# Remainders of the weights and the scale and shift of the input rows on VectorE alone

## The chip, the cores and the metric

The kernel runs on one core of a Trainium2 chip. The metric is the device time of one execution in microseconds (us); the kernel before takes 1100.27 us, the median of three runs (1099.83 to 1100.51). TensorE (PE) multiplies matrices and puts the products into PSUM; VectorE (DVE), ScalarE (ACT) and GpSimd (POOL) work on tiles elementwise; SyncE (SP) issues most DMAs, GpSimd the others.

## The reference

One step of an encoder layer, for 512 prompt tokens and 8 x 16 sample tokens (640 rows of 1024 numbers, all float32):

```
xp = layer_norm(x_prompt, ln_in_g, ln_in_b);  xs = layer_norm(x_sample, ln_in_g, ln_in_b)
mem_k = mem_prompt @ w_mem_k;  mem_v = mem_prompt @ w_mem_v
z = x @ w_in;  xa, ya, glu, q, gates = split(z)
A: h = rg_lru(conv4(xa));                     out_a = (h * gelu(ya)) @ proj_a
B: v = conv31(glu[:512] * sigmoid(glu[512:])); out_b = silu(layer_norm(v)) @ proj_b
C: attention of q over mem_k, mem_v;          out_c = ... @ proj_c
x = layer_norm(alpha * x + (sum_k sigmoid(gate_k) * out_k) @ w_out)
x = layer_norm(alpha * x + (silu(x @ w_gate) * (x @ w_up)) @ w_down)
```

The change touches the first line (the input rows' LayerNorm) and the way in which weights of the second and third lines are prepared.

## The kernel before

A product of two float32 matrices is made of three passes in a faster format. Each operand is split into a high part (a rounded copy, made by ScalarE: `copy`) and a remainder (operand minus high part, made by one `tensor_tensor` with subtract), and TensorE adds high x high, high x remainder and remainder x high. Activations are kept transposed, in `xh` and `xl` (features on partitions, 640 tokens along the row); weights come by DMA into `wr` (two buffers of 1 MB), and each step takes 128 output columns of them, high part in `wh`, remainder in `wl`, 128 x 1024 numbers each.

The program is a list of such steps (`Step`). The loop at the end of `trunk` (L1904 on) goes through them: it prepares the high parts of the two to four steps ahead, then the remainders (`prep_lo`, L301), and emits the matmuls of the step. `prep_lo` uses the engine that the step was given, `self.eng`: VectorE (`V`) as a rule, GpSimd (`G`) for some.

In order, the steps are: eight for the keys and values of the memory (`mem_steps`, L603; 128 x 512 blocks, two to a step), with the LayerNorm and the transposes of the input rows 0 to 639 (five tiles of 128 rows, `xt[0]` to `xt[4]`) put between them by a table `jobs` (L598); then from step 8 on the columns of `w_in`: four steps of GLU, four of queries, four of GLU, eight of `xa`, eight of the third gate; then `proj_c`, and so on. The first three steps of the GLU form a group: their first halves (tokens 0 to 319) run first, then the rest of the input rows is finished (`start_stream`, L557), then their second halves.

An input tile goes through `x_stats` (mean and variance on VectorE, the root on GpSimd), `x_norm` (L533: scale and shift in place; two halves y[0], y[1] of 512 columns), `x_turn` (transposes by TensorE into `pv`) and `x_split` (high part by ScalarE into `xh`, remainder by VectorE into `xl`).

What isn't in the list of steps runs in streams beside it: the convolution of branch B (`conv_b_taps`, 240 instructions of VectorE that read `pb`), its LayerNorm (`ln_b_stream`: GpSimd adds four tiles, `total`, and TensorE sums over the channels with a matrix `ones`), the attention, the recurrence. `advance` decides how much of the streams is emitted between two pieces of matmuls: it lets a stream go on while the planned time of VectorE and ScalarE is behind that of TensorE. The planned times come from prices (`price_vector`, `price_scalar`, `price_tensor`) added up by the wrapper `Engine`. Only VectorE, ScalarE and TensorE have such a wrapper; what GpSimd is given costs nothing in the plan. Each engine then runs its own queue in the order of emission and waits where an operand isn't there.

All instructions that go through the wrapper have line 64 in the profile, so they are told apart by their tiles: `s` is a general slot, `pu` and `pv` are PSUM tiles, `mv`, `rs` and `shift` are numbers of a LayerNorm for each row.

Of the kernel before, what the change touches and what calls it, by code (L numbers as in the profile page):

```python
# [11 lines left out]
OP = mybir.AluOpType  # L12
# [8 lines left out]
HT = T // 2  # L21
KD = D // 128
# [87 lines left out]
class Slots:  # L110
# [7 lines left out]
    def get(self, shape, dtype=F32):  # L118
        if not self.free_list:
            raise RuntimeError("no slot is free")  # L120
        i = self.free_list.pop(0)
        self.low = min(self.low, len(self.free_list))
        self.count += 1
        x = self.pool.tile([128, T], dtype, name=f"s{i}_{self.count}", tag=f"s{i}", bufs=1)
        x = view(x, shape)
        self.at[id(x)] = (i, x)
        return x
# [16 lines left out]
def trunk(ctx, tc, x_prompt, x_sample, mem_prompt, state_conv_a, state_lru, state_conv_b, cache_mem_k, cache_mem_v,  # L144
# [6 lines left out]
    V, A, P = Engine(nc.vector, price_vector), Engine(nc.scalar, price_scalar), Engine(nc.tensor, price_tensor)  # L151
    G, S = nc.gpsimd, nc.sync
# [20 lines left out]
    def pu(n=2):  # L173

        return [ps.tile([128, 512], F32, name="pu", tag="u", bufs=4) for _ in range(n)]
# [3 lines left out]
    def pv():  # L179
        assert side[0] < 2  # L180
        side[0] += 1
        return ps.tile([128, 2, 512], F32, name="pv", tag="v", bufs=2)
# [5 lines left out]
    def over(n=1):  # L188
        side[0] -= n


    def halves_of(p):
        return [p[:, c] for c in range(2)]

    def each(f, out, *a, **k):

        for c in range(2):
            f(c2(out)[:, c], *(x[c] if isinstance(x, list) else x for x in a), **k)

    def two(x):  # L200
        return [c2(x)[:, c] for c in range(2)]
# [16 lines left out]
    loads = []  # L218
# [44 lines left out]
    steps = []  # L263
# [83 lines left out]
    def until(cond):  # L347

        flush()
        for item in list(streams):  # L350
            while not cond():
                try:
                    next(item[1])
                except StopIteration:
                    streams.remove(item)
                    done.add(item[0])
                    break
        assert cond()
# [75 lines left out]
    mem_w = [Blocks(w_mem_k, 0)]  # L434
# [31 lines left out]
    def ln_scale(y, mv, rs):  # L466

        shift = small.tile([128, 1], F32, name="shift")
        V.scalar_tensor_tensor(shift, mv[:, 0:1], -1.0, rs, op0=OP.mult, op1=OP.mult)
        for x in y:  # L470
            A.activation(x, x, AF.Identity, bias=shift, scale=rs)
# [61 lines left out]
    def x_norm(t):  # L533
        g, b = gb_in
        mv, ve, rs = norm.pop(t)
        y = xt[t]
        ln_scale(y[1:], mv, rs)
        V.scalar_tensor_tensor(y[0], y[0], mv[:, 0:1], g[0], op0=OP.subtract, op1=OP.mult)
        V.scalar_tensor_tensor(y[0], y[0], rs, b[0], op0=OP.mult, op1=OP.add)
        G.tensor_tensor(y[1], y[1], g[1], op=OP.mult)  # L540
        G.tensor_tensor(y[1], y[1], b[1], op=OP.add)

    def x_turn(t):
        turning[t] = to_xt(t, xt[t])
# [12 lines left out]
    def start_stream():  # L557
        x_stats(4)
        yield None
        x_norm(4)  # L560
        for t in (3, 4):
            yield None
            yield from room()
            x_turn(t)
            yield None
            x_split(t)
        for r in gb_in:
            free(*r)
# [11 lines left out]
    def mem_evac(which):  # L580
# [8 lines left out]
        else:  # L589
# [5 lines left out]
            for x in memT.values():  # L595
                free(*x)

    jobs = {0: [(mem_turn, 1)], 1: [], 2: [(x_norm, 0)], 3: [(x_turn, 0), (x_stats, 1)],  # L598
            4: [(x_norm, 1), (x_split, 0), (mem_evac, "k"), (x_stats, 2)], 5: [(x_turn, 1), (x_norm, 2)],
            6: [(x_split, 1), (x_turn, 2), (x_stats, 3, False)],  # L600
            7: [(x_root, 3), (x_split, 2), (mem_evac, "v"), (x_norm, 3), (mem_end,)]}

    def mem_steps(which, li):  # L603
        for s in range(4):
            def mm(w, s=s):
                if s == 0:
                    mem_acc[which] = pu()
                p = mem_acc[which]
                for a, b in ((0, 0), (0, 1), (1, 0)):
                    for k in (2 * s, 2 * s + 1):  # L610
                        for m in range(2):
                            P.matmul(p[m], memT[m, k // 4][a][:, k % 4], w[b][:, k % 2], start=(k == 0 and a == b),
                                     stop=(k == KD - 1 and a == 1))
                yield
                for f, *a in jobs[li + s]:
                    f(*a)

            Step(mem_w[li + s], lambda r: r, [128, 2, 512], mm, eng=G if li + s in (3, 5) else V)

    mem_steps("k", 0)  # L620
    mem_steps("v", 4)

    us = {}
# [70 lines left out]
    def fm(p, w, rh, rl, K, cs=(0, 1)):  # L694
        hi, lo = w
        for k in range(K):
            for c in cs:
                P.matmul(p[c][:, :HT], hi[:, k], rh(k, c), start=(k == 0), stop=False)
            for c in cs:
                P.matmul(p[c][:, :HT], hi[:, k], rl(k, c), start=False, stop=False)  # L700
            for c in cs:
                P.matmul(p[c][:, :HT], lo[:, k], rh(k, c), start=False, stop=(k == K - 1))
            if k % 2 == 1:
                yield k % 4 == 1
# [15 lines left out]
    def x_step(ld, o, evac, group=None):  # L720

        def mm(w):
            if group is None:
                s.p = pu()
                yield from fm(s.p, w, xrh, xrl, KD)
                return
            if group[1][0] is s:
                until(lambda: {0, 1, 2} <= turned)
                for z, q in enumerate(group[1]):
                    if z == 2:  # L730
                        until(lambda: side[0] < 2)
                    q.p = pu() if z < 2 else halves_of(pv())
                    yield from fm(q.p, q.w, xrh, xrl, KD, (0,))
                group[0]()
            if s is group[1][-1]:
                over()
            yield from fm(s.p, w, xrh, xrl, KD, (1,))

        s = Step(ld, lambda r: r[:, :, o:o + 128], [128, KD, 128], mm, lambda: evac([x[:, :HT] for x in s.p]),
                 eng=G if ld is loads[0] and o == 0 or 12 <= len(steps) < 36 and len(steps) % 2 else V)  # L740
        if group is not None:
            group[1].append(s)

    def z_step(col, evac, group=None):
        o = col % 256
        x_step(zload[col - o], o, evac, group)
# [984 lines left out]
    for which in ("g", "u"):  # L1731
        for m in range(2):
            def evac(p, m=m, which=which):
                if which == "g":
                    hT[m] = get([128, T])
                    each(A.activation, hT[m], p, AF.Silu)
                else:
                    each(V.tensor_mul, hT[m], two(hT[m]), p)

            x_step(zload[which], m * 128, evac, group=group if len(group[1]) < 3 else None)  # L1740
# [218 lines left out]
```

## Time and profile before

| | |
|---|---|
| median of three runs | 1100.27 us |
| the profiled execution | 1099.67 us |
| its span, first to last instruction | 1097.9 us |
| TensorE busy | 1061.7 us, 97% |
| VectorE busy | 802.9 us, 73% |
| ScalarE busy | 490.1 us, 45% |
| GpSimd busy | 165.3 us, 15% |
| mean granted TensorE clock | 0.99 |

The profile is of one execution. A row of the timeline reads: start in us from the span's start, duration in us, engine, line, operation, output<-inputs, shape, number of instructions merged into the row, and in brackets how long the engine had idled before and what ended that. TensorE's durations overlap (a matmul of 320 columns lasts 0.31 us and the next one starts 0.147 us after it), so its busy time says little; its waits and the granted clock tell where it loses time.

### The profile page before, as it was taken

To read this page: it belongs to the slowest core of one execution; us is meant where nothing else is said; L and a number is where in the kernel's file an instruction comes from. 1 tells how busy PE (TensorE), PEld (TensorE's weight loads), DVE (VectorE), ACT (ScalarE), POOL (GpSimd) and SP (SyncE) were. 2 spreads that over 40 slices of the span, in tenths; PEclk is the share of its full clock that TensorE was granted. 3 is DMA by queue.
4 is the path that set the end of the run, shared out by engine and by line. 5 is a ranking of instruction groups with operands and counts; after the bars stand their busy time and mean duration, and the time that the engine had idled before them with its cause. 6 is when DMAs were issued, how large, how long until landed. Compare 5 with 4: busy or idle time off the path is not lost.

```text
span 1097.9 us, 17000 instructions
## 1 busy us (share of the span) xinstructions
PE 1061.7 (97%) x6827; PEld 1005.9 (92%) x6827; DVE 802.9 (73%) x1335; ACT 490.1 (45%) x863; POOL 165.3 (15%) x185
## 2 busy tenths in 40 slices
PE   8799898998999999999999999899999999999997
PEld 6699898997999999999999889899999999888886
DVE  6929898996364873779855678888887887544775
ACT  4532645446648445846523124433444444334341
POOL 3623323556200000010001120000000000100111
PEclk9999999998999999999999999999999999999999
DMA  9732123352412121212325331132222322734481
GB/s 340 253 95 78 39 67 97 118 154 65 147 52 83 59 96 59 95 45 78 115 78 172 135 134 59 39 101 92 77 78 85 108 77 78 287 115 137 162 289 45
DMA packets 80334, 123.11 MB, mean 112 GB/s; under 512 B 4075, under 2 KB 59371, under 8 KB 80256
## 3 DMA queue, kind: packets, MB, share of 16 engines
q1 hardware_dynamic: 73168, 100.36, 27.6%
q0 software_dynamic: 7088, 21.68, 6.2%
q8 instruction: 53, 0.87, 0.3%
q14 instruction: 25, 0.20, 0.1%
HBM read 112.41 MB, written 9.61 MB: 111 GB/s over the span
## 4 chain that ended last, share of the span: by engine, by line
PE 70%; DVE 11%; ACT 4%; issue 1%; DVEq 0%; ACTq 0%
PE pu L64 62%; DVE s L64 10%; PE pv L64 8%; ACT s L64 3%; ACT L64 1%; DVE wl L64 1%; ACT wh L64 0%; DVE xres L64 0%; DVE mx L64 0%; DVE wh L64 0%; DVE xl L64 0%; DVE nm L64 0%; DVEq L1955 0%; ACT wl L64 0%; DVE st L64 0%
## 5 line engine op out<-in xcount | busy, mean ns | idle before, releaser
L64 PE MATMUL pu<-xh,wh 128*128 128x320 f32 x1040 | 252.6, 315 | 8.3 <-ACT s L64 7.1
L64 PE MATMUL pu<-xh,wl 128*128 128x320 f32 x1040 | 246.9, 310 | 0.0
L64 ACT ACTIVATE wh<-wr 128x1024 fp32r<-128x1024 f32 (+1 forms) x149 | 134.9, 908 | 229.1 <-PE pu L64 123.2
L64 PE MATMUL pu<-xl,wh 128*128 128x320 f32 x888 | 219.7, 311 | 0.0
L64 PEld LDWEIGHTS pu<-xh,wh 128*128 128x128 f32 x1040 | 178.1, 190 | 13.2 <-ACT s L64 9.1
L64 PE MATMUL pu<-s,wh 128*128 128x320 f32 x1064 | 185.5, 310 | 1.9 <-DVE s L64 1.3
L64 PEld LDWEIGHTS pu<-xh,wl 128*128 128x128 f32 x1040 | 177.4, 189 | 0.1
L64 DVE TENSOR_TENSOR s<-s,s 128x640 fp32r<-128x640 f32 (+4 forms) x176 | 124.5, 723 | 65.5 <-ACT s L64 63.3
L64 PEld LDWEIGHTS pu<-s,wh 128*128 128x128 f32 x1064 | 163.4, 188 | 3.4 <-DVE s L64 2.4
L64 DVE TENSOR_TENSOR wl<-wr,wh 128x1024 fp32r<-128x1024 f32 (+1 forms) x100 | 114.1, 1141 | 66.7 <-ACT wh L64 66.7
L64 PEld LDWEIGHTS pu<-xl,wh 128*128 128x128 f32 x888 | 154.2, 189 | 0.6 <-DVE xl L64 0.6
L64 DVE TENSOR_TENSOR s<-s,pu 128x320 f32<-128x320 f32 x188 | 88.4, 484 | 85.8 <-PE pu L64 83.3
L64 PE MATMUL pu<-s,wl 128*128 128x320 f32 x808 | 147.3, 310 | 0.9 <-DVE s L64 0.9
L64 DVE SCALAR_TENSOR_TENSOR s<-s,pb,s 128x511 f32<-128x511 f32 (+14 forms) x240 | 130.1, 613 | 7.8 <-ACT s L64 7.8
L64 ACT ACTIVATE s<-s 128x640 fp32r<-128x640 f32 (+4 forms) x144 | 87.9, 629 | 101.9 <-DVE s L64 101.8
L64 PEld LDWEIGHTS pu<-s,wl 128*128 128x128 f32 x808 | 126.1, 188 | 1.1 <-issue 1.1
L64 PE MATMUL pu<-wh,s 128*128 128x512 f32 (+1 forms) x396 | 116.2, 386 | 0.3 <-ACT wh L64 0.3
L64 PEld LDWEIGHTS pu<-wh,s 128*128 128x128 f32 x396 | 73.1, 189 | 15.1 <-ACT wh L64 1.2
L64 ACT ACTIVATE s<-pu 128x320 f32<-128x320 f32 (+2 forms) x90 | 36.7, 442 | 68.1 <-PE pu L64 68.0
L64 PE MATMUL pu<-wl,s 128*128 128x512 f32 (+1 forms) x198 | 62.9, 389 | 1.6 <-POOL wl L305 0.8
L305 POOL TENSOR_TENSOR wl<-wr,wh 128x1024 fp32r<-128x1024 f32 x13 | 44.4, 3418 | 81.2 <-ACT wh L64 68.4
L64 PE MATMUL pv<-wh,s 128*128 128x512 f32 (+1 forms) x152 | 48.7, 367 | 0.4 <-DVE xres L64 0.4
(139 smaller groups left out, 1249.0 us busy)
## 6 DMA issues: line engine op xcount, KB each, us to landing
wr<-in_w_in SPq DMA_DIRECT2D x26, 1024.0 KB, 5.1
wr<-in_w_ffn_down SPq DMA_DIRECT2D x19, 1024.0 KB, 5.1
wr<-in_w_ffn_gate SPq DMA_DIRECT2D x11, 1024.0 KB, 5.3
wr<-in_w_ffn_up SPq DMA_DIRECT2D x11, 1024.0 KB, 5.3
s<-in_cache_mem_k POOLq DMA_DIRECT2D x16, 256.0 KB, 7.0
s<-in_cache_mem_v POOLq DMA_DIRECT2D x16, 256.0 KB, 7.2
wr<-in_proj_a SPq DMA_DIRECT2D x4, 1024.0 KB
wr<-in_w_out SPq DMA_DIRECT2D x4, 1024.0 KB, 5.7
```

The lines of the kernel that those rows point to most:

```text
L64: return f(*a, **k)
L305: self.eng.tensor_tensor(l, x, f32(h), op=OP.subtract)
```

## The change

Three edits. In `x_norm`, both halves of an input tile are now scaled and shifted by two VectorE instructions each; before, y[1] was scaled by one ScalarE instruction (with a number `shift` that VectorE computes first) and then multiplied by g and added to b by GpSimd. In `mem_steps`, steps 3 and 5 no longer give their remainders to GpSimd. In `x_step`, the first step of `w_in` and the twelve odd steps from 13 to 35 no longer do so either.

```
@@ -534,11 +534,9 @@  x_norm
-        ln_scale(y[1:], mv, rs)
-        V.scalar_tensor_tensor(y[0], y[0], mv[:, 0:1], g[0], op0=OP.subtract, op1=OP.mult)
-        V.scalar_tensor_tensor(y[0], y[0], rs, b[0], op0=OP.mult, op1=OP.add)
-        G.tensor_tensor(y[1], y[1], g[1], op=OP.mult)
-        G.tensor_tensor(y[1], y[1], b[1], op=OP.add)
+        for c in range(2):
+            V.scalar_tensor_tensor(y[c], y[c], mv[:, 0:1], g[c], op0=OP.subtract, op1=OP.mult)
+            V.scalar_tensor_tensor(y[c], y[c], rs, b[c], op0=OP.mult, op1=OP.add)
@@ -615,7 +613,7 @@  mem_steps
-            Step(mem_w[li + s], lambda r: r, [128, 2, 512], mm, eng=G if li + s in (3, 5) else V)
+            Step(mem_w[li + s], lambda r: r, [128, 2, 512], mm)
@@ -736,8 +734,7 @@  x_step
-        s = Step(ld, lambda r: r[:, :, o:o + 128], [128, KD, 128], mm, lambda: evac([x[:, :HT] for x in s.p]),
-                 eng=G if ld is loads[0] and o == 0 or 12 <= len(steps) < 36 and len(steps) % 2 else V)
+        s = Step(ld, lambda r: r[:, :, o:o + 128], [128, KD, 128], mm, lambda: evac([x[:, :HT] for x in s.p]))
```

Since the plan counts VectorE's instructions and not GpSimd's, the streams are also laid out anew between the steps. Three places matter for what follows.

VectorE's queue at memory step 3, before (`s_13_117` and `s_14_118` are the two blocks of that step, done by GpSimd and so not in these rows; `s_7_103` and `s_8_104` are the halves of input tile 0, `s_19_129` is a block of step 4):

```order
L64 TENSOR_TENSOR wl<-s_12_114,wh 128x512
L64 SCALAR_TENSOR_TENSOR shift<-mv,rs 128x1
L64 SCALAR_TENSOR_TENSOR s_7_103<-s_7_103,mv,s_15_121 128x512
L64 SCALAR_TENSOR_TENSOR s_7_103<-s_7_103,rs,s_17_125 128x512
L64 TENSOR_TENSOR wl<-s_19_129,wh 128x512
```

and with the change:

```order
L64 TENSOR_TENSOR wl<-s_12_114,wh 128x512
L64 TENSOR_TENSOR wl<-s_13_117,wh 128x512
L64 TENSOR_TENSOR wl<-s_14_118,wh 128x512
L64 SCALAR_TENSOR_TENSOR s_7_103<-s_7_103,mv,s_15_121 128x512
L64 SCALAR_TENSOR_TENSOR s_7_103<-s_7_103,rs,s_17_125 128x512
L64 SCALAR_TENSOR_TENSOR s_8_104<-s_8_104,mv,s_16_122 128x512
L64 SCALAR_TENSOR_TENSOR s_8_104<-s_8_104,rs,s_18_126 128x512
L64 TENSOR_TENSOR wl<-s_19_129,wh 128x512
```

Both halves of the tile and both blocks of the step now stand in one queue, ahead of the next step's remainders.

ScalarE's queue at the first two softmaxes of the attention, before (rows with `nm` are the exponentials of a row tile, rows with `rc` their scaling, a row into `s` from `pu` empties a step's PSUM tiles, ACT_TABLE_LOAD changes the function table, the row with `pb` starts a convolution):

```order
L64 ACT_TABLE_LOAD
L64 ACTIVATE lam_1261<-lam_1260 128x8
L64 ACTIVATE s_74_1297,sm<-pv,nm 128x256 x2
L64 ACTIVATE s_75_1298,sm<-pv,nm 128x256 x2
L64 ACTIVATE s_76_1316<-s_60_763,pb 128x640
L64 ACT_TABLE_LOAD
L64 ACTIVATE s_77_1326<-pu 128x320 x2
L64 ACTIVATE s_74_1297<-s_74_1297,rc 128x256 x2
L64 ACTIVATE s_75_1298<-s_75_1298,rc 128x256 x2
L64 ACT_TABLE_LOAD
L64 ACTIVATE s_78_1367,sm<-pv,nm 128x256 x2
L64 ACTIVATE s_79_1368,sm<-pv,nm 128x256 x2
```

and with the change, to the row that empties the next step:

```order
L64 ACT_TABLE_LOAD
L64 ACTIVATE lam_1280<-lam_1279 128x8
L64 ACTIVATE s_76_1316,sm<-pv,nm 128x256 x2
L64 ACTIVATE s_77_1317,sm<-pv,nm 128x256 x2
L64 ACTIVATE wh<-wr 128x1024
L64 ACTIVATE s_76_1316<-s_76_1316,rc 128x256 x2
L64 ACTIVATE s_77_1317<-s_77_1317,rc 128x256 x2
L64 ACTIVATE s_78_1379,sm<-pv,nm 128x256 x2
L64 ACTIVATE s_79_1380,sm<-pv,nm 128x256 x2
L64 ACT_TABLE_LOAD
L64 ACTIVATE s_80_1391<-pu 128x320 x2
```

The convolution's start and the emptying of one step now stand ahead of the first exponentials, and one pair of table loads is gone; the whole queue has 19 table loads, before 25.

TensorE's queue where branch B's first channel sums stand (the matmuls with `ones`; `s_162_2714` is the sum of the four convolved tiles made by GpSimd, the rows with `s_95` and `s_96` are score products of the samples), before:

```order
L64 MATMUL pv<-s_160_2700,s_96_1828 32x256
L64 MATMUL pv<-s_161_2702,s_96_1828 32x256
...
L64 MATMUL pv<-s_162_2714,ones 128x512
L64 MATMUL pv<-s_162_2714,ones 128x128
```

and with the change (`s_162_2719` and `s_163_2720` are now probabilities of the samples, `s_155_2619` to `s_158_2622` cached values, `s_181_2871` the sum of the convolved tiles):

```order
L64 MATMUL pv<-ident,s_162_2719 128x128 x4
L64 MATMUL pv<-ident,s_163_2720 128x128 x4
...
L64 MATMUL pv<-s_157_2621,s_179_2854 32x128
L64 MATMUL pv<-s_158_2622,s_179_2854 32x128
L64 MATMUL pv<-s_181_2871,ones 128x512
L64 MATMUL pv<-s_181_2871,ones 128x128
```

The sums stood right behind the score products and now stand behind the samples' softmax and their first value products. Ahead of them TensorE's queue has 1176 matmuls of 320 columns, before 1080. Behind the place where the transposes of `hout` (the end of the recurrence) stood before, TensorE's queue is the same in both programs.

## The prediction

> **What bounds the kernel now.** The page first:
>
> ```profile
> PE 1061.7 (97%) x6827; PEld 1005.9 (92%) x6827; DVE 802.9 (73%) x1335; ACT 490.1 (45%) x863; POOL 165.3 (15%) x185
> DVE  6929898996364873779855678888887887544775
> L305 POOL TENSOR_TENSOR wl<-wr,wh 128x1024 fp32r<-128x1024 f32 x13 | 44.4, 3418 | 81.2 <-ACT wh L64 68.4
> ```
>
> TensorE sets the time: no edit touches its matmuls, so only its waits and slow clock can be won or lost. VectorE's digits are 8 and 9 in slices 2 and 4 to 9 (27 to 247 us, 27.4 us each): there it is nearly full, and there the change adds work to it. The third line is what leaves GpSimd: 13 remainders at 3.42 us. Next, TensorE's waits from 60 to 260 us, and stretches of that time:
>
> ```profile
> PE pv L64 <- POOL s L855: 5.0, 1, 5.0
> PE pu L64 <- ACT s L64: 2.3, 1, 2.3
> PE pu L64 <- DVE s L64: 1.0, 1, 1.0
> ...
> 138.00:142.00 4.00, 4.00 (x19) 4.00 (x18) 4.00 (x7) 1.75 (x5) 3.34 (x1) 0.58 0.00 0
> 220.00:240.00 20.00, 20.00 (x162) 18.47 (x161) 20.00 (x39) 9.98 (x20) 10.76 (x9) 1.00 0.54 159
> 248.00:252.00 4.00, 0.17 (x2) 0.00 (x0) 4.00 (x9) 0.00 (x0) 0.42 (x1) 0.82 0.00 0
> 252.00:256.00 4.00, 2.83 (x7) 1.80 (x7) 2.23 (x3) 2.78 (x8) 4.00 (x5) 0.50 0.34 93
> 256.00:260.00 4.00, 4.00 (x24) 4.00 (x24) 1.76 (x5) 3.97 (x9) 3.46 (x7) 0.83 0.97 288
> ```
>
> (A stretch's columns: length, busy us of PE, PEld, DVE, ACT and POOL with counts, granted clock, DMA share, GB/s.) From 248 us TensorE stands still for 5.0 us: the `ones` matmul waits for GpSimd's sum of the convolved tiles, while VectorE, 20.00 of 20.00 busy before, finishes the last one. Then the clock is at half until about 257.
>
> **What GpSimd's work costs VectorE.** Rows of VectorE in the front, and the undisturbed kind at 32.50 to 34:
>
> ```profile
> 15.74 1.25 DVE L64 SCALAR_TENSOR_TENSOR shift<-mv,rs 128x1 f32<-128x1 f32 x1
> 16.91 1.86 DVE L64 SCALAR_TENSOR_TENSOR s<-s,mv,s 128x512 f32<-128x512 f32 x1
> 18.80 1.66 DVE L64 SCALAR_TENSOR_TENSOR s<-s,rs,s 128x512 f32<-128x512 f32 x1
> 20.39 2.35 DVE L64 TENSOR_TENSOR wl<-s,wh 128x512 fp32r<-128x512 f32 x2
> 25.03 1.23 DVE L64 SCALAR_TENSOR_TENSOR shift<-mv,rs 128x1 f32<-128x1 f32 x1 [0.66 <-POOL rs L463]
> 26.19 1.85 DVE L64 SCALAR_TENSOR_TENSOR s<-s,mv,s 128x512 f32<-128x512 f32 x1
> 28.08 1.67 DVE L64 SCALAR_TENSOR_TENSOR s<-s,rs,s 128x512 f32<-128x512 f32 x1
> 32.50 1.29 DVE L64 TENSOR_TENSOR wl<-s,wh 128x512 fp32r<-128x512 f32 x2
> 33.71 0.15 DVE L64 SCALAR_TENSOR_TENSOR shift<-mv,rs 128x1 f32<-128x1 f32 x1
> 33.78 0.74 DVE L64 SCALAR_TENSOR_TENSOR s<-s,mv,s 128x512 f32<-128x512 f32 x1
> 35.26 3.41 DVE L64 TENSOR_TENSOR wl<-s,wh 128x512 fp32r<-128x512 f32 x2
> 41.43 1.23 DVE L64 TENSOR_TENSOR wl<-wr,wh 128x1024 fp32r<-128x1024 f32 x1
> ```
>
> The same forms take 0.74 us in one place and 1.86 in another, a `shift` of one number a row 0.15 or 1.25. All long ones lie over GpSimd's `wl`, L540 and L541. Their excess: 1.10 + 1.12 + 0.92 + 1.06 + 1.08 + 1.11 + 0.93 + 2.12 = 9.4 us up to 39 us. In the middle (the last row counts only what reads the taps' table `pb`: busy us of DVE and of ACT):
>
> ```profile
> 198.58 3.80 POOL L305 TENSOR_TENSOR wl<-wr,wh 128x1024 fp32r<-128x1024 f32 x1 [11.04 <-ACT wh L64]
> 200.03 2.88 DVE L64 SCALAR_TENSOR_TENSOR s<-s,pb,s 128x495 f32<-128x495 f32 x1
> 204.91 0.72 DVE L64 SCALAR_TENSOR_TENSOR s<-s,pb,s 128x492 f32<-128x492 f32 x1
> 107.83 6.37 DVE L64 SCALAR_TENSOR_TENSOR s<-s,pb,s 128x490 f32<-128x490 f32 x14
> 178.00:252.00 74.00, 67.17 (x120) 1.49 (x2) 0.99 0.45 133
> ```
>
> One remainder on GpSimd holds one tap up by 2.88 - 0.72 = 2.16 us. VectorE does a remainder itself in 1.23 (row 41.43). So for each of these VectorE pays less when it does the work than when GpSimd does. The stretch agrees: 120 taps took 67.2 us; at 6.37/14 = 0.455 they would take 54.6; of the 12.6 us between, four remainders make 4 x 2.16 = 8.6, the rest falls on GpSimd's own adds, which stay.
>
> The page "Perfetto Trace Analysis" of the Trainium skill ("Optimizing Scalar/DVE Operations") says that with VectorE saturated, offloading to ScalarE or even GpSimd may make sense; the change does the reverse in a full stretch. It adds that between GpSimd and VectorE this may not help because of a shared read port; the rows above bear out the second half.
>
> **The change, part by part.** The sum is made against the profiled execution's 1099.67 us (span 1097.9 and 1.8 around it), which is 0.6 us below the runs' median.
>
> *A, the front (to 58 us).*
>
> ```profile
> 38.17 0.66 PE L64 MATMUL pv<-ident,s 128*128 128x128 f32 x4 [2.09 <-POOL s L541]
> 38.00:40.00 2.00, 1.83 (x8) 1.58 (x9) 2.00 (x4) 1.70 (x3) 2.00 (x2) 0.73 0.98 327
> 40.00:42.00 2.00, 2.00 (x6) 1.52 (x6) 1.93 (x5) 0.00 (x0) 1.35 (x2) 0.50 0.74 276
> 43.31 0.41 PE L64 MATMUL pu<-xl,wh 128*128 128x320 f32 x1
> 49.98 0.66 PE L64 MATMUL pv<-ident,s 128*128 128x128 f32 x4 [0.84 <-POOL s L541]
> 54.90 1.37 PE L64 MATMUL pv<-ident,s 128*128 128x128 f32 x8 [0.74 <-DVE xl L64]
> 57.87 0.31 PE L64 MATMUL pu<-xh,wh 128*128 128x320 f32 x1
> ```
>
> VectorE is full from 14.5 us, and the first matmul with `xl` (43.31) waits for it. Its queue up to there gains two pairs of blocks (2 x 1.29), two 0.75 instructions for each of tiles 0 to 2 (4.5) and one remainder (1.23): 8.3 us. It loses the excess, 9.4, and three `shift`s, 0.4. Net -1.5: the `xl` matmul at 41.8. ScalarE's and GpSimd's lost work there (five of each) lay beside VectorE's and gives no more. TensorE now reaches that matmul early: its memory steps no longer wait for L541, tile 2's second half is ready near 34.7 rather than at 38.1 (VectorE's queue again), and transposes and the last step take 3.9 us from there, so they end near 38.6 and TensorE idles some 3 us. A wait of 2.09 us (row 38.17) was followed by 3.4 us of half clock, 1.7 us lost; I charge 1.3 of the same here, part of it lying inside the wait. From the `xl` matmul to the second halves' start was 57.87 - 43.31 = 14.6 us, with waits of 0.84 at 49.98 and 0.74 at the next tile. The first goes: behind the `xl` pair VectorE has one more pair and tile 3's four instructions, 1.3 + 3.0 us, done by 47. The second grows: with the new order no matmuls stand between tile 4's transposes and the second halves, so ScalarE's copy and VectorE's remainder of its first half are waited for in full, about 0.6 us each (half of the pair's 1.29, and as much for the copy), 0.4 more than before. 41.8 + 1.3 + 14.6 - 0.84 + 0.4 = 57.2 against 57.87: **A = -0.7**; bounds -2.5 (no half clock, tile 4 hidden) and +1.5 (a second half-clock period at tile 4).
>
> "TensorE: Matmul & The Clock Gate" of the Trainium skill (Part 1) gives at least one idle window of about 3.4 us before the clock halves. By that rule the idle 3 us need not halve it and A would be -2.0. The row after 2.09 us of waiting speaks against counting on it, so the charge stays.
>
> *B, the stop at 248 us.* GpSimd's adds, and from the chain of work a stretch of matmuls without waits (start, us, count):
>
> ```profile
> L855 POOL TENSOR_TENSOR s<-s,s 128x640 f32<-128x640 f32 x4 | 6.7, 1674 | 11.1 <-DVE s L64 8.1 <-ACT s L64 2.9
> 293.90 12.32 PE pu L64 x84
> ```
>
> The stop is 5.0 us of wait and, from its end at 253.2 to about 257, half clock on some 3.6 us, 1.8 us. With the change the `ones` matmul stands 96 matmuls of 320 columns later in TensorE's queue, 96 x 12.32/84 = 14 us. VectorE in the same stretch has 4 x (2.16 - 1.23) = 3.7 us less to do, and 2 x 1.23 = 2.5 us more for the two steps that now fall into it. So the last tap is done before TensorE arrives. What is late next is GpSimd's three adds, 1.7 us each: before, two were done ahead of the last tap; now all stand behind it, and there are 3.5 us of matmuls plus the transposes and value products between emission and use, where 5.1 are needed. I leave 1.5 us of wait, below the 2.09 that is followed by half clock. **B = -5.0 - 1.8 + 1.5 = -5.3**; bounds -6.8 and 0.
>
> *C, 107 us.* The 1.0 us wait for a VectorE row stands behind taps lengthened by GpSimd's remainder of 100.5 us. **C = -1.0**; bounds -1.0 and 0.
>
> *D, 137 us.*
>
> ```profile
> 130.85 1.28 ACT L64 ACT_TABLE_LOAD   x1 [0.48 <-DVE nm L64]
> 133.96 1.07 ACT L64 ACTIVATE wh<-wr 128x1024 fp32r<-128x1024 f32 x1
> 136.82 0.74 PE L64 MATMUL pu<-xh,wh 128*128 128x320 f32 x2 [2.30 <-ACT s L64]
> ```
>
> TensorE waits 2.3 us until ScalarE, after two softmaxes with a table load between, empties the step's PSUM; half clock follows (0.58 from 138 to 142), 1.7 us. In the new queue the load at 130.85 (1.28) and the copy at 133.96 (1.07) no longer stand in that chain: 2.35 us, as much as the wait. **D = -4.0**; bounds -4.0 and 0, since the softmax keeps its place on ScalarE and a wait may return there.
>
> *E, VectorE's new work elsewhere.* Eleven remainders at 1.23 us join its queue from 60 to 285 us. Where it has room, they lie beside matmuls; at a softmax or the emptying of a step one may stand ahead of what TensorE waits for. I charge one, **+1.2**; bounds -2 (small waits go, as VectorE is freer) and +5 (four in the full stretch, as in the rival below). Weight buffers come free sooner, which hides nothing, since no matmul waits there for a weight's DMA.
>
> Sum: -0.7 - 5.3 - 1.0 - 4.0 + 1.2 = -9.8: **1089.9 us**; the case's own range is 1084 to 1095.
>
> **The rivals.**
> 1. *The stop moves.* The wait of B returns on GpSimd's adds (5 us behind the last tap, half clock again), or D's returns at another softmax. For it: both have a new neighbour that is nearly as late. Against: neither wait needs VectorE's backlog any more. Time: 1089.9 + 4.0 to 5.3, about 1094.5.
> 2. *Both return.* 1089.9 + 9.3 = 1099.2, no difference. That the change did nothing by itself, because GpSimd wasn't in the way, would end there too; the 0.74 against 1.86 speaks against it.
> 3. *VectorE becomes the bound.* In the full stretch 180 to 250 us four remainders at 1.23 stand ahead of taps and of the emptying of steps, with nothing given back: 4.9 us more, 1104.6, slower. It decides if a tap beside a remainder shrinks by less than 1.23 us; the 2.16 measured, and 14 us more room in TensorE's queue, speak against. The rule on a saturated VectorE in "Perfetto Trace Analysis" (the Trainium skill), cited above, would come out this way.
>
> **How the numbers follow.** Forecast 0.55, rival 1 0.20, rival 2 0.10, rival 3 0.15. A measurement of this kernel can tell about 0.2% (2.2 us) from no change: forecast and rival 1 are faster, 0.75; rival 2 same, 0.10; rival 3 slower, 0.15. The low end takes the terms' best bounds but part of E: 1099.7 - 2.5 - 6.8 - 1 - 4 - 2 = 1083.4. The high end, 1101, takes in rivals 1 and 2 and leaves out most of rival 3.
>
> **What would show it.** Right: VectorE's busy time near the old one (26 us added: 13 remainders at 1.23, 4 at 0.65, ten instructions of 0.75; gone the 9.4 and about ten times 2.16), taps of 0.72 everywhere but under GpSimd's adds; the `xl` matmul near 41.8; a wait below 2 us at `ones`; no half clock near 137 and 250; the second halves starting near 57. Wrong: forms of 0.74 us still taking 1.8 with GpSimd idle; `ones` waiting 3 us or more; new waits of TensorE for VectorE's `s` or `wl` between 60 and 260 us, or clock halved at 55.

## The result and the profile after

| | before | after |
|---|---|---|
| median, us | 1100.39 (four runs, 1099.83 to 1101.31) | 1083.04 (four runs, 1080.89 to 1084.34) |
| profiled execution, us | 1099.67 | 1080.89 |
| its span, us | 1097.9 | 1078.8 |

The ratio is 0.9841, 95% interval 0.9828 to 0.9854: 17.3 us faster. The forecast was 1089.9, with a range from 1083.4 to 1101: the gain is larger than forecast, and the time lies 0.4 us below the range. The profiled execution is the fastest of the four.

From the page of after, the busy times of the engines, VectorE's digits and the group of the convolution's taps:

```profile
PE 1052.7 (98%) x6827; PEld 1002.7 (93%) x6827; DVE 798.6 (74%) x1357; ACT 479.4 (44%) x852; POOL 107.8 (10%) x158
DVE  6939989988377747877545678888878887545775
L64 DVE SCALAR_TENSOR_TENSOR s<-s,pb,s 128x511 f32<-128x511 f32 (+14 forms) x240 | 112.6, 540 | 2.8 <-ACT s L64 2.8
```

The same group on the page of before:

```profile
L64 DVE SCALAR_TENSOR_TENSOR s<-s,pb,s 128x511 f32<-128x511 f32 (+14 forms) x240 | 130.1, 613 | 7.8 <-ACT s L64 7.8
```

VectorE has 22 instructions more, 13 of them remainders of 1.2 us, and yet is busy for 4.3 us less; the 240 taps alone took 17.5 us less. From 178 to 252 us the taps now read (busy us of VectorE second, with its count):

```profile
178.00:252.00 74.00, 52.28 (x111) 0.92 (x1) 1.00 0.51 151
```

That is 0.471 us for one, against 67.17/120 = 0.560 before. TensorE's waits between 60 and 300 us in after (total us, times, longest):

```profile
PE pv L64 <- ACT s L64: 1.4, 2, 0.9
PE pu L64 <- ACT s L64: 0.6, 1, 0.6
PE pu L64 <- DVE s L64: 0.4, 1, 0.4
```

and the stretch from 100 to 200 us in after:

```profile
100.00:200.00 100.00, 100.00 (x718) 99.90 (x717) 93.34 (x200) 52.88 (x142) 27.45 (x49) 1.00 0.36 109
```

In before the same list of waits, the lines that the prediction did not show:

```profile
PE pv L64 <- DVE s L64: 2.6, 3, 1.6
...
PE pv L64 <- ACT s L64: 1.1, 1, 1.1
```

and the same stretch in before:

```profile
100.00:200.00 100.00, 92.93 (x639) 90.81 (x638) 89.99 (x181) 51.65 (x136) 29.62 (x43) 0.98 0.22 67
```

Between 100 and 200 us TensorE no longer waits at all: 718 matmuls where there were 639, and a granted clock of 1.00 where it was 0.98. The places that the prediction named, in after's timeline:

```profile
41.66 0.42 PE L64 MATMUL pu<-xl,wh 128*128 128x320 f32 x1 [3.33 <-DVE xl L64]
...
55.25 0.41 PE L64 MATMUL pu<-xh,wh 128*128 128x320 f32 x1 [0.69 <-ACT xh L64]
56.46 0.42 PE L64 MATMUL pu<-xl,wh 128*128 128x320 f32 x1 [0.81 <-DVE xl L64]
...
234.48 2.02 POOL L852 TENSOR_TENSOR s<-s,s 128x640 f32<-128x640 f32 x1
248.35 4.04 POOL L852 TENSOR_TENSOR s<-s,s 128x640 f32<-128x640 f32 x1 [11.85 <-DVE s L64]
```

and the `ones` matmuls among after's instructions by tile (shortest, median and longest ns, first and last start us):

```profile
L64 PE MATMUL pv<-s,ones x4: 273/434/697, 253.3 to 254.3; 128*128 128x512 f32 x2, 128*128 128x128 f32 x2
```

The first matmul with `xl` waits 3.33 us; the `ones` matmuls start 0.9 us after GpSimd's last add has ended (248.35 + 4.04) and wait for nothing.

Where the time was gained is seen by pairing the k-th matmul of 320 columns into `pu` of two traces and taking the difference of their starts. Between 240 and 480 us the pairing is disturbed, since other matmuls moved across these, so columns are taken outside of it. At 119 us the kernels with the order of after (all rows but e1) have 12 matmuls of 256 columns still to come that before has behind it, about 1.5 us of what they show there; in the other columns the matmuls ahead are the same. The kernels of the experiments below are in the same table.

| us gained, at the time in before | 64 | 119 | 205 | 235 | 491 | 930 |
|---|---|---|---|---|---|---|
| after | 1.7 | 6.2 | 12.7 | 12.7 | 18.9 | 19.1 |
| e1: VectorE does the work, order of before | 1.5 | 2.8 | 5.7 | 5.8 | 9.3 | 9.7 |
| e2: GpSimd does the work, order of after | -0.3 | 4.2 | 10.6 | 3.3 | 3.7 | 4.0 |
| e10: e2 with one remainder on VectorE | 0.1 | 4.6 | 11.0 | 11.0 | 10.9 | 11.6 |
| e4: the twelve odd steps alone | -0.1 | 4.4 | 10.8 | 10.8 | 17.0 | 17.6 |
| e5: after, with idle subtractions on GpSimd | -0.9 | 3.6 | 8.2 | 8.2 | 3.0 | 2.0 |

After gains 1.7 us in the front, 11.0 from 64 to 205 us, 6.4 behind that. The middle is the surprise: its forecast was C + D + E = -3.8.

### The profile page after: what moved, and what is told of

It reads as the page before. It is cut to its first block, busy times and chain, and to the rows that moved or that the text cites. A ratio compares the mean times of both kernels' runs of the same rounds, so it can differ in the third digit from the quotient of the medians.

```text
span 1078.8 us, 16991 instructions
## 1 busy us (share of the span) xinstructions
PE 1052.7 (98%) x6827; PEld 1002.7 (93%) x6827; DVE 798.6 (74%) x1357; ACT 479.4 (44%) x852; POOL 107.8 (10%) x158
## 4 chain that ended last, share of the span: by engine, by line
PE 54%; DVE 1%; ACT 0%; issue 0%; DVEq 0%; ACTq 0%
PE pu L64 48%; PE pv L64 6%; DVE s L64 1%; DVE xres L64 0%; ACT s L64 0%; ACT wh L64 0%; DVEq L1952 0%; ACT wl L64 0%; DVE st L64 0%; DVE mv L64 0%; DVE ve L64 0%; DVE wl L64 0%; ACTq L64 0%; DVEq L64 0%
## 5 line engine op out<-in xcount | busy, mean ns | idle before, releaser
L64 DVE TENSOR_TENSOR wl<-wr,wh 128x1024 fp32r<-128x1024 f32 (+1 forms) x113 | 130.1, 1152 | 62.6 <-ACT wh L64 62.5
L64 DVE SCALAR_TENSOR_TENSOR s<-s,pb,s 128x511 f32<-128x511 f32 (+14 forms) x240 | 112.6, 540 | 2.8 <-ACT s L64 2.8
L64 PE MATMUL pv<-s,s 128*32 128x128 f32 (+4 forms) x420 | 45.8, 308 | 1.4 <-ACT s L64 1.4
```

Of the source, the lines that this page charges most:

```text
L64: return f(*a, **k)
```

## The experiments

The change does two things at once: another engine does the work, and the plan, which counts VectorE's instructions and not GpSimd's, lays out the streams anew. Theory 1: the gain comes from VectorE no longer being held up by GpSimd's subtractions. Theory 2: it comes from the new order. The first two kernels separate them. Times are medians; the ratio with its 95% interval is against runs of before on the same chip (medians 1099.9 to 1100.0).

| | us | ratio |
|---|---|---|
| e1_vector_old_layout | 1090.22 | 0.9917 (0.9902 to 0.9932) |
| e2_gpsimd_new_layout | 1095.51 | 0.9965 (0.9953 to 0.9977) |
| e3_norm_only | 1100.55 | 1.0012 (1.0003 to 1.0022) |
| e4_odd_steps_only | 1081.95 | 0.9839 (0.9823 to 0.9856) |
| e5_idle_subtractions | 1096.51 | 0.9962 (0.9948 to 0.9975) |
| e6_idle_memsets | 1083.80 | 0.9850 (0.9834 to 0.9867) |
| e7_front_order | 1081.44 | 0.9830 (0.9816 to 0.9845) |
| e9_gpsimd_keys_by_sync | 1096.72 | 0.9967 (0.9955 to 0.9978) |
| e10_one_remainder_back | 1087.73 | 0.9889 (0.9872 to 0.9905) |

**e1: the engine alone.** VectorE does all of it, but past the wrapper that counts its time, so that TensorE's queue is that of before:

```
-            Step(mem_w[li + s], lambda r: r, [128, 2, 512], mm)
+            Step(mem_w[li + s], lambda r: r, [128, 2, 512], mm, eng=nc.vector if li + s in (3, 5) else V)
...
+                 eng=nc.vector if ld is loads[0] and o == 0 or 12 <= len(steps) < 36 and len(steps) % 2 else V)
...
+        V.time += 130 + 1 / 0.96
+        A.time += 130 + 512 / 1.2 + 2 * 93
+            v = nc.vector if c else V
+            v.scalar_tensor_tensor(y[c], y[c], mv[:, 0:1], g[c], op0=OP.subtract, op1=OP.mult)
+            v.scalar_tensor_tensor(y[c], y[c], rs, b[c], op0=OP.mult, op1=OP.add)
```

> VectorE does all remainders and both halves of every input tile, but the plan is charged as before, so TensorE's and ScalarE's queues are those of the kernel before (ScalarE without its five scalings). Hold-up theory (GpSimd's instructions stretch VectorE's, and TensorE waits for the stretched ones): nearly the whole gain comes with the engine alone, 1083 to 1087 us. Layout theory (the streams placed later between the steps win the time): VectorE's rows shorten, but the waits stay where they stood; only the front's 1 to 2 us go, 1096 to 1099 us.

Measured: 1090.22 us, 9.1 of the 17.3 us by the ratio, between the two ranges expected. Two of TensorE's waits in its timeline:

```profile
134.66 0.74 PE L64 MATMUL pu<-xh,wh 128*128 128x320 f32 x2 [2.95 <-ACT s L64]
...
243.87 1.35 PE L64 MATMUL pv<-s,ones 128*128 128x512 f32 x4 [1.46 <-POOL s L856]
```

all of TensorE's waits from 100 to 200 us:

```profile
PE pu L64 <- ACT s L64: 3.0, 1, 3.0
PE pv L64 <- DVE s L64: 1.2, 2, 0.9
```

and its taps from 178 to 252 us:

```profile
178.00:252.00 74.00, 54.20 (x113) 0.92 (x1) 1.00 0.50 151
```

The taps are as short as in after. The stop at `ones` shrinks from 5.0 to 1.46 us. From 100 to 200 us TensorE waits for 4.2 us, 7.0 in before: the waits of before at 107 (0.98), 169 (1.15) and 188 us (1.62) are gone. But the wait of term D is still there, longer than the 2.30 before: taking GpSimd out of VectorE's way does not remove it.

**e2: the order alone.** GpSimd and ScalarE keep their work, and its time is added to the plan as if VectorE did it, so that TensorE's queue is that of after:

```
+    class GV:
+        @staticmethod
+        def tensor_tensor(*a, **k):
+            V.time += price_vector(V, "tensor_tensor", a, k)
+            return G.tensor_tensor(*a, **k)
...
+            Step(mem_w[li + s], lambda r: r, [128, 2, 512], mm, eng=GV if li + s in (3, 5) else V)
...
+                 eng=GV if ld is loads[0] and o == 0 or 12 <= len(steps) < 36 and len(steps) % 2 else V)
...
+        V.time += 2 * (130 + 512 / 0.96)
```

> GpSimd and ScalarE keep their work as before, but the plan is charged as in the changed kernel, so TensorE's queue is the changed kernel's. Hold-up theory: the stretched rows stay, 1095 to 1102 us. Layout theory: 1084 to 1089 us. If both shares are needed, this run and the first one add up to more or less than the 17 us together.

Measured: 1095.51 us, 3.8 us by the ratio. That lies in the range expected of theory 1. Its trace shows why the number is small, and it is not for stretched rows of VectorE alone. First the stretch from 100 to 200 us:

```profile
100.00:200.00 100.00, 100.00 (x717) 99.90 (x717) 92.13 (x194) 53.24 (x145) 45.22 (x51) 1.00 0.30 94
```

then rows of TensorE, GpSimd and VectorE in its timeline:

```profile
227.58 1.09 PE L64 MATMUL pv<-ident,s 128*128 128x128 f32 x4 [4.76 <-DMA s<-in_cache_mem_k]
...
265.14 1.94 PE L64 MATMUL pv<-s,s 128*32 128x128 f32 x32 [5.06 <-ACT s L64]
...
203.79 18.37 POOL L158 TENSOR_TENSOR wl<-wr,wh 128x1024 fp32r<-128x1024 f32 x1 [6.99 <-PE pv L64]
222.10 2.99 POOL L1078 DMA_DIRECT2D s<-in_cache_mem_k  x4
...
202.28 16.47 DVE L64 SCALAR_TENSOR_TENSOR s<-s,pb,s 128x488 f32<-128x488 f32 x36
```

Up to 205 us the order alone gains 10.6 us, nearly what after has there (12.7, of which 1.7 came in the front), although GpSimd still does its subtractions. Then two waits of about 5 us come. By the table the first takes back 7.3 us (from 10.6 to 3.3); the second stands where before has its own stop of 5.0 us, so that nothing is won there. One GpSimd remainder lasts 18.37 us; during it VectorE runs 36 taps at 16.47/36 = 0.457 us, not held up at all, and the loads of cached keys that GpSimd issues stand behind it.

**e3 and e4: which of the edits.** e3 has only the edit in `x_norm`, e4 only the one that gives the twelve odd steps from 13 to 35 to VectorE.

```
-                 eng=G if ld is loads[0] and o == 0 or 12 <= len(steps) < 36 and len(steps) % 2 else V)
+                 eng=G if ld is loads[0] and o == 0 else V)
```

> Only the scale and shift of the input rows goes to VectorE; remainders stay on GpSimd. Hold-up theory: the front loses five scalings and ten GpSimd instructions, so 1 to 2 us go before 64 us, and all later waits stay: 1097 to 1100 us. Layout theory: the plan moves little, the same time; this run tells what share the front has, not which theory holds.

> Only the twelve odd steps from 13 to 35 give their remainders to VectorE; the front is the kernel before's. Both theories: the 15 us between 64 and 300 us go, the front's 2 us stay: 1083 to 1087 us. If it is above 1092 us, the front's edits also work behind 64 us.

Measured: e3 1100.55, no gain and just above its range; e4 1081.95, the whole gain and 1 us below its range. TensorE's waits from 60 to 300 us in e4:

```profile
PE pv L64 <- ACT s L64: 1.4, 2, 0.9
PE pu L64 <- ACT s L64: 0.6, 1, 0.6
```

They are those of after but for one of 0.4 us. The front edits bring nothing measurable: up to 60 us VectorE is busy for 45.72 us in before and for 45.40 in after, so what the hold-ups cost there, its new work costs again.

**e5 and e6: the hold-up by itself.** To after are added, at each of the twelve odd steps, instructions of GpSimd whose result nobody uses: two subtractions of 128 x 512 in e5, six memsets of 128 x 512 in e6.

```
+            i = steps.index(self)
+            if 12 <= i < 36 and i % 2:
+                for k in range(2):
+                    G.tensor_tensor(scr, f32(xh[:, k, :512]), f32(xl[:, k, :512]), op=OP.subtract)
...
+    scr = one.tile([128, 512], F32, name="scr")
```

> The changed kernel, with two extra GpSimd subtractions of 128x512 at each of the twelve odd steps (operands xh and xl, result never read): GpSimd is as busy as before, nobody waits for it, queues and plan of the other engines are the changed kernel's. Hold-up theory: VectorE's rows lengthen again (24 times about 1.1 us) or GpSimd's do, and the late GpSimd DMAs and adds come later: 1086 to 1094 us. If the time lay only in waiting for GpSimd's results: 1082 to 1085 us, as the changed kernel.

> The same, with six memsets of 128x512 (0.53 us each, 3.2 us a step) in the place of the two subtractions: GpSimd is busy as long but reads nothing. If VectorE is held up by any GpSimd instruction, as in the run with subtractions. If it is held up only by those that read two tiles, VectorE's rows stay short and the time is the changed kernel's within 2 us.

Measured: e5 1096.51, 13.5 us above after and above the range expected; e6 1083.80, as after. GpSimd's group of the added instructions from 60 to 300 us (busy us, mean ns, idle time before them) in e5:

```profile
L309 POOL TENSOR_TENSOR scr<-xh,xl 128x512 f32<-128x512 f32 x21 | 33.6, 1598 | 1.2
```

e5's taps from 178 to 252 us:

```profile
178.00:252.00 74.00, 63.73 (x110) 0.92 (x1) 0.96 0.51 153
```

and in e5's timeline VectorE's row that gives the softmax of the samples its maximum, with ScalarE and TensorE behind it:

```profile
248.63 0.17 DVE L64 TENSOR_SCALAR nm<-mx 128x4 f32<-128x4 f32 x1
...
248.88 1.28 ACT L64 ACT_TABLE_LOAD   x1 [12.81 <-DVE nm L64]
...
254.00 1.05 PE L64 MATMUL pu<-xh,wh 128*128 128x320 f32 x2 [10.50 <-ACT s L64]
```

The same table load in after:

```profile
234.51 1.28 ACT L64 ACT_TABLE_LOAD   x1 [2.93 <-DVE nm L64]
```

The group of the added instructions in e6:

```profile
L309 POOL MEMSET scr<- 128x512 f32 x62 | 32.7, 528 | 3.2
```

and e6's taps:

```profile
178.00:252.00 74.00, 54.33 (x116) 0.92 (x1) 1.00 0.49 146
```

GpSimd is busy for as long in both (33.6 and 32.7 us). Beside the subtractions a tap takes 63.73/110 = 0.579 us, beside the memsets 54.33/116 = 0.468, in after 0.471. Subtractions of SBUF tiles hold VectorE up, memsets don't. In the full stretch the delay adds up until ScalarE idles 12.81 us for `nm`, where it idles 2.93 in after, and TensorE stands for 10.50 us.

The Trainium skill, page "SBUF — State Buffer", section "Who interferes with whom", says that a VectorE instruction with two inputs in SBUF contends with a GpSimd instruction that reads SBUF, not with one that only writes it. e5 and e6 agree: 0.579 and 0.468 us.

**e7: the front's wait.** After, with tile 3's statistics and the remainder of step 9 moved behind tile 2's split, so that `xl` is ready earlier.

```
-            6: [(x_split, 1), (x_turn, 2), (x_stats, 3, False)],
-            7: [(x_root, 3), (x_split, 2), (mem_evac, "v"), (x_norm, 3), (mem_end,)]}
+            6: [(x_split, 1), (x_turn, 2)],
+            7: [(x_split, 2), (lambda: steps[9].prep_lo(),), (x_stats, 3), (mem_evac, "v"), (x_norm, 3), (mem_end,)]}
...
-            while new:
+            while new and not (i == 7 and len(new) == 1):
```

> The changed kernel with tile 3's statistics and step 9's remainder put behind the xl pair of tile 2 in VectorE's queue (same work, same TensorE queue). The 3.3 us wait for xl at 41.7 us shrinks to under 1 us. If that wait is what the front loses: 1079 to 1081 us. If VectorE's sum of work up to the second halves bounds the front, the wait returns at step 10's remainder or tile 4, and the time is 1081 to 1084 us, but for the half-clock period that a 3.3 us wait brings in some executions.

Measured: 1081.44 (1080.52 to 1082.47). In its timeline:

```profile
38.93 0.41 PE L64 MATMUL pu<-xl,wh 128*128 128x320 f32 x1 [0.55 <-DVE xl L64]
49.27 0.41 PE L64 MATMUL pv<-xh,wl 128*128 128x320 f32 x1 [1.86 <-DVE wl L64]
...
55.86 0.41 PE L64 MATMUL pu<-xh,wh 128*128 128x320 f32 x1 [0.69 <-ACT xh L64]
```

and a stretch of the front (the granted clock is the third number from the end):

```profile
50.00:54.00 4.00, 4.00 (x19) 4.00 (x19) 3.34 (x5) 0.00 (x0) 3.90 (x8) 0.57 0.93 331
```

The wait of 3.33 us is gone, another of 1.86 us for VectorE comes at the next step, as in the second outcome expected, and the second halves start at 55.86, in after's profiled execution at 55.25. But half clock followed the new wait (0.57 from 50 to 54 us), so this trace doesn't show whether VectorE's sum alone bounds the front. Its median is 1.6 us below after's, 0.15%, which these runs don't tell from no change.

**e9 and e10: what takes back the gain of e2.** e9 is e2 with the loads of cached keys and values issued by SyncE, so that they don't stand behind GpSimd's remainders.

```
-                G.dma_start(to[h][i], rows[:, 4 * i:4 * i + 4, h])
+                S.dma_start(to[h][i], rows[:, 4 * i:4 * i + 4, h])
```

> GpSimd keeps the work, the plan is the changed kernel's (the second run), and the DMAs of the cached keys and values are issued by SyncE. The second run's 4.8 us wait for a cached key stood behind one GpSimd remainder of 18.4 us. If the queue behind that remainder is the cause: the wait goes, 1086 to 1091 us. If the transfer itself was late, or SyncE's queue holds it as long, 1094 to 1098 us.

Measured: 1096.72, no better than e2, and TensorE still waits for the keys: the second of the two outcomes expected. TensorE, SyncE's queue and GpSimd in its timeline:

```profile
228.18 1.94 PE L64 MATMUL pv<-ident,s 128*128 128x128 f32 x8 [5.36 <-DMA s<-in_cache_mem_k]
...
194.26 3.76 SPq L1078 DMA_DIRECT2D s<-in_cache_mem_k  x4
222.19 0.37 SPq L265 DMA_DIRECT2D wr<-in_w_in  x1
222.60 3.22 SPq L1078 DMA_DIRECT2D s<-in_cache_mem_k  x4
...
203.78 18.38 POOL L158 TENSOR_TENSOR wl<-wr,wh 128x1024 fp32r<-128x1024 f32 x1 [13.32 <-PE pv L64]
```

SyncE issues nothing from 198 to 222.19 us. The weight load at its head writes a buffer `wr`, and the long remainder reads one until 203.78 + 18.38 = 222.16, just before the load goes out. By these times the keys stand behind the same instruction on either queue. e10 tries this: e2, with only that one remainder (step 29) given to VectorE; all queues are else in the same order.

```
-                 eng=GV if ld is loads[0] and o == 0 or 12 <= len(steps) < 36 and len(steps) % 2 else V)
+                 eng=GV if ld is loads[0] and o == 0 or 12 <= len(steps) < 36 and len(steps) % 2 and len(steps) != 29 else V)
```

> As e2_gpsimd_new_layout, but the remainder of one step, the one that lasted 18.37 us on GpSimd at 203.79, is made by VectorE; the order of all queues is else the same. Theory (the stop at 227 us comes from that one long subtraction, which holds up the issue of the cached keys on GpSimd's own queue, and with the keys on SyncE's queue holds up SyncE through the weight buffer): the keys go out before 215 us, the wait of 4.76 us for in_cache_mem_k is gone, the next GpSimd remainder at 228 is ordinary, and the time is 1086 to 1090 us (1095.5 - 4.8 - 1.7 of half clock - up to 3 of what follows). Rival (the keys are late since the streams are emitted too late whatever GpSimd does, or another remainder starves in its place): a wait of over 3 us for in_cache_mem_k stays between 220 and 235, and the time is 1094 to 1097 us.

Measured: 1087.73, 7.8 us below e2, from one instruction. In its timeline:

```profile
201.38 0.75 POOL L1078 DMA_DIRECT2D s<-in_cache_mem_k  x1 [1.63 <-DMA s<-in_cache_mem_k]
204.99 2.96 POOL L1078 DMA_DIRECT2D s<-in_cache_mem_v  x4 [2.86 <-ACT s L64]
223.34 10.46 POOL L158 TENSOR_TENSOR wl<-wr,wh 128x1024 fp32r<-128x1024 f32 x1 [15.38 <-ACT wh L64]
...
257.52 1.94 PE L64 MATMUL pv<-s,s 128*32 128x128 f32 x32 [5.10 <-ACT s L64]
```

The keys go out by about 202 us and the wait for them is gone. The next remainder was expected to be an ordinary one and took 10.46 us; the second wait of e2 stays (5.10 us). That one makes up most of the 5.8 us between e10 and e4, which has the same work but no GpSimd remainder in the full stretch; the chain that leads to it through VectorE and ScalarE was not tried apart.

## Where the prediction was right, and where it failed

The direction was right, and so was the hold-up: GpSimd's subtractions cost VectorE more than the work itself does. Eight of them lie in e5's stretch from 178 to 252 us, and against e6 its taps lose about 110 x (0.579 - 0.468) = 12 us there, 1.5 us for each, where VectorE makes two such blocks in 1.29. The stop at 248 us hung on VectorE's backlog (5.0 us in before, 1.46 in e1); the other large one, D's, did not. None of the rivals came: no stop returned, and VectorE did not become the bound, since the taps shrank by more than the remainders add. The sum was too small by 9.3 us against the span of the profiled execution (1097.9 - 1078.8 = 19.1 gained, 9.8 forecast), and the time by 6.9 us against the median, in these terms:

*A, the front: forecast -0.7, measured -1.7 in the profiled execution.* The `xl` matmul came at 41.66 (forecast 41.8) after 3.33 us of idleness (some 3). The half clock that was charged with 1.3 us did not follow in this execution, whose granted clock was 1.00 up to 60 us. That was luck: e6's profiled execution has the same front and the same wait, and there it followed. e6's `xl` matmul, the stretch behind it in e6, and the same stretch in after:

```profile
41.68 0.64 PE L64 MATMUL pu<-xl,wh 128*128 128x320 f32 x1 [3.33 <-DVE xl L64]
42.00:46.00 4.00, 4.00 (x16) 4.00 (x16) 3.86 (x7) 0.00 (x0) 0.00 (x0) 0.50 0.97 299
42.00:46.00 4.00, 4.00 (x29) 4.00 (x28) 3.86 (x7) 0.00 (x0) 0.00 (x0) 1.00 1.02 293
```

Paired with before as in the table, e6 is 0.3 us behind at 64 us, where after is 1.7 ahead: the half clock, charged with 1.3 us, costs about 2.0. The other three executions of after were 1.8 to 3.5 us longer, at a mean granted clock of 0.992 to 0.993 against 0.996; where they lost it was not recorded. On the median the front is worth nothing: e4, without the front edits, has the same ratio as after (0.9839 and 0.9841).

*B, the stop at 248: forecast -5.3, measured about -6.4.* The wait was placed right, but 1.5 us were left for GpSimd's adds, on the ground that all three would stand behind the last tap. Only the last one did (248.35); the first two ran at 232.85 and 234.48. e1 splits the term: the engine takes the wait from 5.0 to 1.46, the order takes the rest.

*C and D: forecast -1.0 and -4.0; both waits are gone.* C's wait goes with the engine alone (e1), as said, and with the order alone (e2) as well. D's reason holds: with the engine alone (e1) the wait is still 2.95 us, with the order alone (e2) TensorE has no wait at all from 100 to 200 us. It was the order, as said; whether the place of the table load or of the copy did it was not tried apart.

*E, VectorE's new work elsewhere: forecast +1.2, bounds -2 and +5; measured about -6.0* (11.0 gained from 64 to 205 us, less the 5.0 of C and D). This is the step that failed, in size and in sign. It looked for what eleven more remainders might delay, and took "small waits go" to be worth at most 2 us. The waits view of before had 2.6 us for `s` of VectorE and 1.1 us for `s` of ScalarE beside C's and D's, 3.7 us, in lines that the prediction passed over; all of it went. The other 2.3 us were lost in the first matmuls behind the waits, C's and D's among them. Behind C's wait in before, and three pairs further on:

```profile
107.56 0.81 PE L64 MATMUL pu<-xh,wh 128*128 128x320 f32 x2 [0.98 <-DVE s L64]
108.80 0.46 PE L64 MATMUL pu<-xh,wh 128*128 128x320 f32 x2
```

A pair lasts 0.81 us there instead of 0.46. Taken from start to start between 64 and 205 us, before has 10.8 us beyond the usual distance of the same matmuls (those more than 0.1 us longer): 7.1 of waiting, about 1.4 of half clock behind D's wait, and 2.3 in such slow starts; after has none.

The reason was only in part the one that E considered, a freer VectorE. With the engine alone (e1) 4.2 us are gained from 64 to 205 us, 3.2 besides C's, more than the 2 that E allowed; with the order alone (e2), GpSimd's work unchanged, 10.9 are, as much as in after. By the plan's rule the streams wait longer, as VectorE's planned time now holds the remainders, and their work stands further behind what TensorE waits for, as the `ones` matmuls do by 96 matmuls; which of the moved rows removes which wait was not tried apart. The prediction followed the new order at the three places that it quoted and charged the rest by VectorE's load alone.

So order and engine each are worth something alone, 3.8 and 9.1 us, and together 17.3: the order gains 10.6 by 205 us, and e2 loses 7.3 of it behind the one remainder that holds up the keys. With that one on VectorE (e10) it is kept, and the 6 us of the stop at 248 us come on top when no GpSimd remainder runs in the full stretch (e4).

The rule of the Trainium skill ("Perfetto Trace Analysis", "Optimizing Scalar/DVE Operations") that a saturated VectorE may be relieved by another engine would have given the slower outcome. With GpSimd as that engine these runs show the reverse, 1095.51 us with the work on GpSimd (e2) and 1083.04 without (after), TensorE's order being the same; they bear out its caution that this may not help between the two.

## What to carry to other kernels

Where a planner prices only some engines, moving work to a priced engine is two changes, the engine and the order: make each alone before explaining a gain. An elementwise instruction with two SBUF inputs put on GpSimd beside a full VectorE is not free: ask what it adds to VectorE's queue, what stands behind it on GpSimd, and which buffer it holds. Add up all the small waits of the bounding engine in the stretch that is laid out anew, not only the large ones.

## What the runs showed of the hardware

The hold-up goes either way. In before, one GpSimd remainder made a tap 2.16 us longer; in e2 one was itself stretched to 18.37 us while 36 taps ran past it at 0.457 us each, and in e9 it happened again at the same place (18.38). What decides who waits was not found.

TensorE's clock halved after 2.09 us of waiting in before and after 1.86 us in e7. After the wait of 3.33 us at 41.7 us it halved in e6's profiled execution (0.50) and did not in after's (1.00). The Trainium skill, "TensorE: Matmul & The Clock Gate" (Part 1), has the clock judged in free-running windows of about 3.4 us, so that the place of a wait in the window matters; the two executions with the same wait agree with that. Waits shorter than a whole such window were enough here, and no run here shows the windows themselves.
